# Program order on all four compute engines until the projections end, with three pieces of work one step later

## The chip, the cores and the metric

The kernel runs on one core of a Trainium2 chip. The metric is the device time of one launch in microseconds (us), as the median over several runs. The engines are TensorE (PE, matmuls; its weight loads are listed as PEld), VectorE (DVE), ScalarE (ACT), GpSimd (POOL) and SyncE (SP), whose queue issues nearly all transfers.

## The reference

One encoder layer over two sequences (256 and 2048 tokens, each with 16 learned meta tokens ahead). With z the input, in float32:

```python
h = rmsnorm(z, norm_w)
q, k, v, g_att, c_val, c_glu, g_conv = split(h @ w_in)      # 512,128,128,512,512,512,512
q, k = rmsnorm per head (64 wide)
att = windowed_gqa(q, k, v, sink) * silu(g_att)             # 8 heads, 2 KV heads, window 128, ALiBi, sink
cnv = conformer_conv(c_val, c_glu, ...) * silu(g_conv)      # GLU, depthwise conv of 31, layernorm, silu
y = z + concat(att, cnv) @ w_out
```

Each block of 128 queries sees its own block of keys, the block before and the one after, and the 16 meta keys. The meta tokens' own outputs are dropped.

## The kernel before

**Blocks and precision.** The 2304 tokens are 18 blocks of 128 (2 of the short sequence, 16 of the long one), in six groups of three. Float32 products are made of two parts: each operand is split into a high half (a cast on ACT) and a low half (a subtraction on DVE), and a product takes three matmuls (high x high, high x low, low x high).

**Stage 1, projections.** Two chunks of three groups. For each chunk the columns of `w_in` are taken unit by unit (256 columns): the convolution's units, its gate, the attention gate, keys and values, then two units of q. The last unit of the second chunk is q's second half for blocks 9 to 17: nine projections of 24 matmuls each (`proj_te`, L790 to L804; the matmul is L796). Each is followed by `head_norm` (L892: a squaring on ACT, L897; a sum on DVE, L898; two POOL instructions at L122 and L123 that make the reciprocal root `rqq`), and by `fin` in `q_group` (L914: DVE multiplies by `rqq`, L916, and a store to DRAM follows two ticks later). The convolution's taps on DVE and a layernorm for it are worked off beside the projections and are done before this last unit.

**Stage 2, attention and output.** Attention runs in steps `(s, slot)`, eight slots for each block (`slot_step`, L567). A slot issues: a bank of four transposes of finished probabilities (`bank`, L433, of the block before), two output products (`outproj`, from slot 14 on), and one pair of score matmuls S (`scores`, L354). Behind S come, one tick later, the bias and row minimum on DVE (`bias_max`, L382), two ticks later the exponential on ACT (`expo`, L394), and after the fourth S of a KV head, three ticks later, `norm` (DVE L406 and L407, POOL L408 and L417). A bank is split by ACT (L451, `ph`) and DVE (L452, `pl`) one tick later, and multiplied with V (`pv`, L475) two ticks later; `pvm` and `pd` in the text are the product with the meta values and POOL's operand for it (L462). `merge` puts the results together; it waits until `rest` exists, a tile that takes the place of the last projection weights.

**The clock of ticks.** `later(k, f)` appends f to a list that is run k ticks on; `tick()` ends a projection or a slot, and runs what is due, in the order in which it was appended. So the Python program fixes an emission order for every engine.

**The overlap, around the change.** `attention_open()` (L218) is called ahead of the last unit, when block 9's projection is next. It opens the pools of stage 2, loads q, k, bias, sink and the first `w_out` rows, clears three tiles on POOL, and computes `nsnk` from the sink on DVE (L250). Then `spread(b)` (L600) runs after each of the nine projections: after the second it issues `q_prep(0)` (transposes of q, tagged qT; the split by ACT L347, L348 and DVE L349, L350 a tick later); after each of the third to ninth it runs two slots, 14 in all: the eight of block 0, then the first six of block 1, with block 0's banks. After the third to the eighth it calls `split_wo`, which casts two halves of a row block of `w_out` on ACT (L301), subtracts on DVE (L302) and a tick later loads the row block two further on (L287).

**What sets the order.** The scheduler orders each engine's instructions at build time by its own estimate of when each is ready, unless told otherwise. `manual_schedule(engines)` makes the named engines issue what is emitted within it in emission order. From `attention_open()` on to the end of the projections this holds for `MAN1`, which is POOL alone; afterwards for `MAN2`, POOL and PE. `keep_in_program_order` pins a single instruction behind the one emitted before it on its engine. SP's queue is the scheduler's throughout.

**PSUM.** Four tags of two buffers each. The nine last projections take tags a, b, d, c, d, c, d, c, d; S takes a, transposes take b, attention's products c, output products d.

Of the kernel before, what the change touches and what calls it, by code (L numbers as in the profile page):

```python
# [14 lines left out]
ALU = mybir.AluOpType  # L15
# [31 lines left out]
W0 = 3  # L47
LN_WAIT = (9, 2)
LTAGS = "abdcdcdcd"
MAN1 = {mybir.EngineType.Pool}  # L50
MAN2 = {mybir.EngineType.Pool, mybir.EngineType.PE}
QSLOT = 6
MSLOT = 0
# [22 lines left out]
def hymba_kernel(  # L76
# [13 lines left out]
    nc = tc.nc  # L90
# [45 lines left out]
    def later(k, f):  # L136
        due.setdefault(clock[0] + k, []).append(f)
# [34 lines left out]
    phase = [1]  # L172
# [40 lines left out]
    pool, cst, kw, wo, wo_slot, sbs, wraws = {}, {}, [], {}, {}, [], {}  # L213
# [4 lines left out]
    def attention_open():  # L218
# [4 lines left out]
        cst['man'] = man  # L223
        man.enter_context(tc.manual_schedule(engines=MAN1))
        ap = att_pools.enter_context(tc.tile_pool(name="ap", bufs=2, side="right", reuse_waits="tile"))
# [57 lines left out]
    def load_raw(n):  # L283

        for nh in range(2):
            raw = wraws[n, nh] = pool["a"].tile([P, 512], F32, tag="woraw", name=f"woraw{n}_{nh}", bufs=4)
            tc.keep_in_program_order(nc.sync.dma_start(raw, w_out[OUT_ORDER[n]][:, 512 * nh : 512 * nh + 512]))  # L287

    def split_wo(n):

        e = OUT_ORDER[n]
        for hl in range(2):
            idx = 2 * n + hl
            if idx % 3 == 0:
                slot = idx // 3
                wo_slot[slot] = xp.tile([P, ND, 400], F32R, tag=("xh", "xl")[slot % 2], name=f"wo{slot}")
            flat = wo_slot[idx // 3].rearrange("p a n -> p (a n)")
            wo[e, hl] = flat[:, D * (idx % 3) : D * (idx % 3) + D]
        for nh in range(2):
            hi, lo = (wo[e, hl][:, 512 * nh : 512 * nh + 512] for hl in range(2))  # L300
            tc.keep_in_program_order(nc.scalar.copy(hi, wraws[n, nh]))  # L301
            tc.keep_in_program_order(nc.vector.tensor_tensor(lo, wraws[n, nh], hi, op=ALU.subtract))  # L302
        if n + 2 < 8:
            later(1, lambda: load_raw(n + 2))

    def load_ga(b):
        gat[b] = pool["b"].tile([P, 4, P], F32, tag="ga", name=f"ga{b}", bufs=1)
# [28 lines left out]
    def q_prep(b):  # L336
        pt = psum.tile([P, 4, P], F32, tag="b", name=f"qT{b}")
        for j in range(4):
            pin(b == 0 and j == 0)(nc.tensor.transpose)(pt[:, j, :], qt[b][:, j, :], ident)
        q2 = pool["a"].tile([P, 4, 4, 2, QB], F32R, tag="q2", name=f"q2_{b}")  # L340
        q2t[b] = q2
        later(1, lambda: q_split(pt, q2))
# [83 lines left out]
    def plan(b):  # L426
        ks = ([0] if has_left(b) else []) + [1] + ([2] if has_right(b) else [])
        return [(k, 0) for k in ks] + [("m", 0)] + [(k, 1) for k in ks]
# [4 lines left out]
    def bank(b, k, kv):  # L433
        pt = psum.tile([P, 4, P], F32, tag="b", name=f"pT{b}_{k}_{kv}")
        if k == "m":
            for i in range(KV):
                nc.tensor.transpose(pt[:, i, :], pmt[b][:, i].rearrange("p a h m -> p (a h m)"), ident)
        else:
            for hl in range(4):
                nc.tensor.transpose(pt[:, hl, :], sbt[b, kv][:, hl, KCOL[k] : KCOL[k] + P], ident)  # L440

        def split():
            if k == "m":
                ph = pool["a"].tile([P, KV, P], F32R, tag="phm", name=f"phm{b}", bufs=1)
                nc.scalar.copy(ph, pt[:, 0:KV, :])
                nc.vector.tensor_tensor(ph[64:128], pt[64:128, 0:KV, :], ph[64:128], op=ALU.subtract)  # L446
                later(1, lambda: spread_meta(b, ph))
                return
            ph = pool["a"].tile([P, 4, P], F32R, tag="ph", name=f"ph{b}_{k}_{kv}", bufs=3)
            pl = pool["a"].tile([P, 4, P], F32R, tag="pl", name=f"pl{b}_{k}_{kv}", bufs=3)  # L450
            nc.scalar.copy(ph, pt)  # L451
            nc.vector.tensor_tensor(pl, pt, ph, op=ALU.subtract)  # L452
            pv_st[b, k, kv] = (ph, pl)

        later(1, split)
        later(3 if k == "m" else 2, lambda: pv(b, k, kv))

    def spread_meta(b, ph):

        pd = pool["a"].tile([P, KV, 4, P], F32R, tag="pd", name=f"pd{b}", bufs=1)  # L460
        for kv in range(KV):
            nc.gpsimd.tensor_tensor(  # L462
                pd[:, kv],
                ph[:, kv : kv + 1, :].to_broadcast([P, 4, P]),
                cst["msk"].unsqueeze(2).to_broadcast([P, 4, P]),
                op=ALU.mult,
            )
        pv_st[b, "m"] = pd

    def pv_mm(b, kv, lhs, hs, start, stop):  # L470
        if start:
            opj[b, kv] = psum.tile([P, 4, P], F32, tag="c", name=f"O{b}_{kv}")
        o = opj[b, kv]
        for i, t in enumerate(hs):
            nc.tensor.matmul(o, lhs, t, start=(start and i == 0), stop=(stop and i == 1))  # L475

    def pv_meta(b, kv, stop):
        pin(stop)(nc.tensor.matmul)(
            opj[b, kv], cst["vm"][:, kv, :], pv_st[b, "m"][:, kv], start=False, stop=stop
        )  # L480

    def pv(b, k, kv):
        if k == "m":
            pv_meta(b, 0, True)
            later(1, lambda: merge(b, 0))
            return
        ks = [x for x, y in plan(b) if y == kv and x != "m"]
        first, last = k == ks[0], kv == 1 and k == ks[-1]
        pv_mm(b, kv, vt[b - 1 + k][:, kv, :], pv_st[b, k, kv], first, last)
        if kv == 1 and first:  # L490
            pv_meta(b, 1, False)
        if last:
            later(1, lambda: merge(b, 1))

    def merge(b, kv):
        if "rest" not in cst or (kv == 1 and b not in att):
            return later(1, lambda: merge(b, kv))
        o = opj[b, kv]
        if kv == 0:
            att[b] = pool["b"].tile([P, 4, P], F32, tag="at", name=f"at{b}")  # L500
            mix[b, 1] = (rest_part(2 * (b % 2)), rest_part(2 * (b % 2) + 1))
        at = att[b]
        pr = slice(2 * kv, 2 * kv + 2)
        tmp = pool["b"].tile([64, 4, P], F32, tag="tmp", name=f"tmp{b}_{kv}", bufs=1)
        nc.scalar.copy(tmp, o[64:128])
        for par in range(2):
            nc.vector.tensor_tensor(
                at[64 * par : 64 * par + 64, pr, :].rearrange("p a (i q) -> p a i q", q=QB),
                o[0:64].rearrange("p i (a c q) -> p c a i q", a=2, c=2)[:, par],
                tmp.rearrange("p i (a c q) -> p c a i q", a=2, c=2)[:, par],  # L510
                op=ALU.add,
            )
        nc.gpsimd.tensor_tensor(at[:, pr, :], at[:, pr, :], gat[b][:, pr, :], op=ALU.mult)

        def fin():
            mh, ml = mix[b, 1]
            nc.scalar.copy(mh[:, pr, :], at[:, pr, :])
            nc.vector.tensor_tensor(ml[:, pr, :], at[:, pr, :], mh[:, pr, :], op=ALU.subtract)

        later(2, fin)  # L520
# [77 lines left out]
    spread_n = [0]  # L598

    def spread(b):  # L600

        spread_n[0] += 1
        if spread_n[0] == QP:
            q_prep(0)
        upto = EARLY * max(0, spread_n[0] - QP) // (9 - QP)
        while len(slots) > len_all - upto:
            slot_step(*slots.pop(0))
        if 3 <= spread_n[0] <= 8:
            split_wo(spread_n[0] - 3)
        if spread_n[0] == 4:  # L610
            load_mix(0)
        if spread_n[0] == 5:
            load_ga(0)
# [21 lines left out]
    if True:  # L635
# [273 lines left out]
        def q_group(ws, qi, g, after):  # L909
            for b in range(3 * g, 3 * g + 3):  # L910
                ps = proj_te(ws, g, blk_local(b)[1], P)
                rq = head_norm(ps, P, 4, f"q{qi}_{b}")

                def fin(ps=ps, rq=rq, b=b):  # L914
                    qs = gp.tile([P, 4, HD], F32, tag="qs", name=f"qs{qi}_{b}")
                    nc.vector.tensor_tensor(  # L916
                        qs,
                        ps[:, :UW].rearrange("p (h e) -> p h e", e=HD),
                        rq.unsqueeze(2).to_broadcast([P, 4, HD]),
                        op=ALU.mult,  # L920
                    )
                    store(qd[b, :, UW * qi : UW * qi + UW], qs.rearrange("p h e -> p (h e)"))

                owe(340)
                later(1, fin)
                tick(24 * 110)
                after(b)

# [132 lines left out]
        for i, (c, u, g) in enumerate(items):  # L1061
# [36 lines left out]
            if c == 0 and u in U_GA:  # L1098
                for k3 in range(3):
                    k = 10 + 3 * (3 * (u - U_GA[0]) + g) + k3  # L1100
# [78 lines left out]
```

## Time and profile before

| | us |
|---|---|
| median of 3 runs | 977.79 (976.96 to 979.07) |
| profiled execution | 974.97 |
| its span | 972.8 |
| PE busy in the span | 947.0 (97%) |
| DVE busy | 754.1 (78%) |
| ACT busy | 422.5 (43%) |
| POOL busy | 340.6 (35%) |

The profile shows one execution. Its page lists busy time, a strip of 40 slices of 24.3 us with the busy share of each engine in tenths and the granted TensorE clock, the chain of work that ended last, and the costliest groups of instructions. By the chain of work PE holds 92% of the span; the chain is made of projections (L780, L796), output products (L551) and the attention's matmuls. A timeline row gives start, duration, engine, line and operation, and in brackets how long the engine stood idle before it and what released it. A row of waits gives total, count and longest.

The nine projections of the last unit begin at about 576 us and the last one ends at 616 us.

### The profile page before, as it was taken

The numbers are of one execution on the slowest core, as the hardware profiler recorded it, in microseconds if no ns is written. First come the engines' busy times: TensorE is split into PE (matmuls) and PEld (weight loads), VectorE is DVE, ScalarE is ACT, GpSimd is POOL, SyncE is SP. The second block draws the span as 40 slices with busy tenths as digits, with TensorE's granted clock in tenths as the row PEclk, the third lists the DMA queues.
The fourth block names the chain that finished last, engine by engine and source line by source line (L and its number), as shares of the span: only waits on it lengthen the run. The fifth ranks groups of instructions, "written<-read, shape, count | busy, mean of one in ns | idle before, by whom it ended". The sixth has DMA issues, their size and how long they took to land.

```text
span 972.8 us, 16221 instructions
## 1 busy us (share of the span) xinstructions
PE 947.0 (97%) x5721; PEld 886.3 (91%) x5721; DVE 754.1 (78%) x1261; ACT 422.5 (43%) x1156; POOL 340.6 (35%) x541
## 2 busy tenths in 40 slices
PE   5999999999999999999999998899999999999998
PEld 4999999999999999999999998678888888888886
DVE  4659999998977799999993555867777677767773
ACT  7521121343566710111113455656666666656661
POOL 5600000364467300000002443855445444445442
PEclk9999999999999999999999998999999999999999
DMA  9653354775635221233335639854555445544422
GB/s 332 229 188 117 117 178 172 265 287 189 225 123 174 76 91 74 86 128 136 127 135 179 207 111 258 257 156 126 166 163 164 125 148 170 171 135 127 138 78 76
DMA packets 113872, 155.75 MB, mean 160 GB/s; under 512 B 10592, under 2 KB 77296, under 8 KB 113792
## 3 DMA queue, kind: packets, MB, share of 16 engines
q1 hardware_dynamic: 113648, 154.11, 48.1%
q0 software_dynamic: 144, 0.62, 0.4%
q8 instruction: 45, 0.74, 0.3%
q14 instruction: 35, 0.29, 0.1%
HBM read 101.00 MB, written 54.31 MB: 160 GB/s over the span
## 4 chain that ended last, share of the span: by engine, by line
PE 92%; DMA 2%; DVE 2%; SPq 1%; POOL 1%; issue 1%; ACT 1%; DVEq 0%; POOLq 0%; ACTq 0%
PE pj L780 42%; PE y L551 20%; PE pj L796 14%; PE O L475 5%; PE pT L440 4%; PE S L327 3%; PE O L327 1%; PE lnt L184 1%; DMA wraw<-in_w_in 1%; PE lnu L203 1%; PE qT L327 1%; DMA v<-vd 1%; DMA qd<-qs 1%; DVE wo L302 0%; DVE sb L382 0%
## 5 line engine op out<-in xcount | busy, mean ns | idle before, releaser
L780 PE MATMUL pj<-xh,ws 128*128 128x384 f32 (+1 forms) x1536 | 396.9, 339 | 2.4 <-ACT xh L711 2.4
L863 DVE SCALAR_TENSOR_TENSOR y<-us,cw,y 128x1167 f32<-128x1167 f32 x240 | 328.9, 1425 | 0.6
L780 PEld LDWEIGHTS pj<-xh,ws 128*128 128x128 f32 x1536 | 282.4, 189 | 2.7 <-ACT xh L711 2.7
L780 PE MATMUL pj<-xl,ws 128*128 128x384 f32 (+1 forms) x768 | 262.0, 341 | 0.0
L551 PE MATMUL y<-wo,rest 128*128 128x512 f32 x648 | 173.6, 405 | 0.0
L796 PE MATMUL pj<-ws,xh 128*128 128x256 f32 (+1 forms) x880 | 165.6, 286 | 2.2 <-ACT es L403 1.4
L780 PEld LDWEIGHTS pj<-xl,ws 128*128 128x128 f32 x768 | 144.8, 189 | 0.6 <-DVE xl L720 0.5
L796 PEld LDWEIGHTS pj<-ws,xh 128*128 128x128 f32 (+1 forms) x880 | 137.5, 189 | 3.5 <-ACT sb L394 1.6
L551 PEld LDWEIGHTS y<-wo,rest 128*128 128x128 f32 x648 | 115.2, 189 | 20.4
L796 PE MATMUL pj<-ws,xl 128*128 128x256 f32 (+1 forms) x440 | 125.0, 284 | 0.0
L394 ACT ACTIVATE sb<-sb,nm 128x304 f32<-128x304 f32 (+4 forms) x144 | 77.1, 535 | 63.6 <-DVE nm L382 61.7
L452 DVE TENSOR_TENSOR pl<-pT,ph 128x512 fp32r<-128x512 f32 x100 | 68.5, 685 | 31.8 <-ACT ph L451 31.0
L888 ACT ACTIVATE go<-pj 128x384 f32<-128x384 f32 x48 | 23.6, 491 | 153.9 <-PE pj L780 143.9
L382 DVE CUSTOM_DVE_ANT_0 sb<-S,bias,small 128x304 f32<-128x304 f32 (+4 forms) x144 | 73.1, 511 | 16.0 <-PE S L327 14.9
L796 PEld LDWEIGHTS pj<-ws,xl 128*128 128x128 f32 (+1 forms) x440 | 83.2, 189 | 0.2
L122 POOL TENSOR_SCALAR ssk<-ssk 128x2 f32<-128x2 f32 x18 | 6.4, 354 | 210.9 <-ACT sqk L902 210.8
L417 POOL TENSOR_SCALAR sb<-sb,es 128x304 f32<-128x304 f32 (+4 forms) x144 | 72.1, 519 | 3.5
L451 ACT CAST ph<-pT 128x512 fp32r<-128x512 f32 x100 | 58.0, 581 | 32.8 <-PE pT L440 32.0
L327 PEld LDWEIGHTS S<-kw,q 128*128 128x128 f32 x288 | 53.0, 188 | 13.1 <-DVE nm L382 1.4
L327 PE MATMUL S<-kw,q 128*128 128x304 f32 (+4 forms) x288 | 61.9, 299 | 0.6 <-DVE nm L382 0.6
L440 PE MATMUL pT<-ident,sb 128*128 128x128 f32 x400 | 60.4, 272 | 1.2 <-DVE phm L446 1.1
L122 POOL TENSOR_SCALAR ssq<-ssq 128x4 f32<-128x4 f32 (+2 forms) x55 | 26.4, 480 | 98.1 <-ACT xn L649 76.7
(118 smaller groups left out, 1280.5 us busy)
## 6 DMA issues: line engine op xcount, KB each, us to landing
wd<-ws SPq DMA_DIRECT2D x36, 512.0 KB, 5.7
ws<-wd SPq DMA_DIRECT2D x36, 512.0 KB, 5.3
wraw<-in_w_in SPq DMA_DIRECT2D x52, 256.0 KB, 5.9
xn<-in_z SPq DMA_DIRECT2D x18, 512.0 KB, 5.4
gd<-go SPq DMA_DIRECT2D x48, 192.0 KB, 2.3
yo<-in_z SPq DMA_DIRECT2D x36, 256.0 KB, 4.5
out_y<-yo SPq DMA_DIRECT2D x36, 256.0 KB, 2.7
kw<-kd SPq DMA_DIRECT2D x16, 512.0 KB, 4.6
```

Source lines behind the costliest of these rows:

```text
L327: r = f(*a, **k)
L382: nc.vector.tensor_tensor_reduce(out=sb[:, n, c0:c1], in0=ps[:, 0:w], in1=cst["bias"][:, kv, n, c0 - QB * n : c1 - QB * n], scale=1.0, sca ...
L394: nc.scalar.activation(sb[:, n, c0:c1], sb[:, n, c0:c1], AF.Exp, bias=nm[:, n : n + 1], scale=-1.0, accum_out=rs[:, n : n + 1],)
L417: nc.gpsimd.tensor_scalar(sb[:, k, a0:a1], sb[:, k, a0:a1], es[:, k : k + 1], 1.0, op0=ALU.mult, op1=ALU.mult)
L440: nc.tensor.transpose(pt[:, hl, :], sbt[b, kv][:, hl, KCOL[k] : KCOL[k] + P], ident)
L451: nc.scalar.copy(ph, pt)
L452: nc.vector.tensor_tensor(pl, pt, ph, op=ALU.subtract)
L475: nc.tensor.matmul(o, lhs, t, start=(start and i == 0), stop=(stop and i == 1))
L551: nc.tensor.matmul(ps, mh[mi][:, e % 4, :], wo[e, wi][:, cols], start=(e == 4 and k == 0), stop=(e == 3 and k == 2),)
L780: nc.tensor.matmul(ps[:, :n], ws[:, d, wi, P * half_i : P * half_i + P], x[xi][:, d, o : o + n], start=(k == 0), stop=(k == 3 * ND - 1),)
L796: nc.tensor.matmul(ps[:rows, :UW], x[xi][:, d, o : o + rows], ws[:, d, wi, :], start=(k == 0), stop=(k == 3 * ND - 1),)
L863: nc.vector.scalar_tensor_tensor(y[:, yo + o0 : yo + o1], u[:, o0 + k : o1 + k], cw[:, j, k : k + 1], y[:, yo + o0 : yo + o1], op0=ALU.mul ...
```

## The change

`MAN1` becomes all four compute engines, so that from `attention_open()` until the projections end PE, ACT, DVE and POOL all issue in emission order. Four pieces of work are moved in that order:

- In `split_wo` the low half of the first 512 columns is emitted one tick after the cast and that of the second two ticks after; the next load of `w_out` rows is emitted with the second low half. In `spread`, `split_wo` is called ahead of the two slots instead of behind them.
- The products of block 0's probabilities with V (`pv`) come three ticks after the bank instead of two.
- In `q_group`, `fin` comes `phase[0]` ticks after the projection: one as before in the earlier units, two in the last unit, where `phase[0]` is 2.

```diff
-MAN1 = {mybir.EngineType.Pool}
+MAN1 = {getattr(mybir.EngineType, e) for e in ("Pool", "PE", "Activation", "DVE")}
...
             tc.keep_in_program_order(nc.scalar.copy(hi, wraws[n, nh]))
-            tc.keep_in_program_order(nc.vector.tensor_tensor(lo, wraws[n, nh], hi, op=ALU.subtract))
-        if n + 2 < 8:
-            later(1, lambda: load_raw(n + 2))
+
+            def low(nh=nh, hi=hi, lo=lo):
+                tc.keep_in_program_order(nc.vector.tensor_tensor(lo, wraws[n, nh], hi, op=ALU.subtract))
+                if nh == 1 and n + 2 < 8:
+                    load_raw(n + 2)
+
+            later(1 + nh, low)
...
-        later(3 if k == "m" else 2, lambda: pv(b, k, kv))
+        later(3 if k == "m" or b == 0 else 2, lambda: pv(b, k, kv))
...
         upto = EARLY * max(0, spread_n[0] - QP) // (9 - QP)
+        if 3 <= spread_n[0] <= 8:
+            split_wo(spread_n[0] - 3)
         while len(slots) > len_all - upto:
             slot_step(*slots.pop(0))
-        if 3 <= spread_n[0] <= 8:
-            split_wo(spread_n[0] - 3)
...
-                later(1, fin)
+                later(phase[0], fin)
```

## The prediction

> **What bounds the kernel now.** I read the strip of 40 slices first, then busy time by stretch, then waits by engine, then the timeline of the stretch that stood out.
>
> ```profile
> PE   5999999999999999999999998899999999999998
> DVE  4659999998977799999993555867777677767773
> PEclk9999999999999999999999998999999999999999
> ```
>
> ```profile
> 577.00:597.00 20.00, 20.00 (x173) 20.00 (x172) 6.44 (x18) 8.55 (x20) 9.35 (x30) 1.00 0.67 186
> 597.00:617.00 20.00, 15.49 (x91) 13.25 (x90) 15.09 (x48) 14.20 (x45) 7.16 (x14) 0.83 1.02 329
> 617.00:637.00 20.00, 15.01 (x72) 11.15 (x71) 17.84 (x37) 13.05 (x31) 14.84 (x19) 0.91 0.64 192
> 637.00:657.00 20.00, 19.91 (x109) 16.76 (x108) 13.28 (x38) 11.57 (x33) 11.04 (x19) 1.00 0.50 145
> ```
>
> The columns are stretch, length, then busy time of PE, weight loads, DVE, ACT and POOL, the granted clock, DMA share and GB/s. PE bounds the program. Its one weak place is 597 to 637: it is idle 4.51 + 4.99 = 9.5 us and the clock falls. That is exactly the stretch that the change reorders. Afterwards PE is full, so the end moves by what PE loses before 637, and by nothing else.
>
> ```profile
> PE pj L796 <- ACT es L403: 1.4, 1, 1.4
> PE pT_m L437 <- POOL pm L408: 2.1, 1, 2.1
> 597.00:599.00 2.00, 0.68 (x7) 0.48 (x5) 1.38 (x3) 1.36 (x5) 0.00 (x0) 1.00 0.85 223
> 599.00:601.00 2.00, 1.74 (x10) 1.20 (x10) 2.00 (x10) 1.33 (x4) 0.00 (x0) 1.00 0.98 259
> 601.00:603.00 2.00, 0.84 (x4) 0.46 (x3) 0.45 (x4) 1.96 (x6) 0.00 (x0) 0.57 1.02 277
> 603.00:605.00 2.00, 1.81 (x8) 1.84 (x9) 2.00 (x7) 2.00 (x10) 0.00 (x0) 0.50 1.01 341
> 633.00:635.00 2.00, 0.55 (x3) 0.15 (x2) 2.00 (x7) 0.55 (x3) 0.00 (x0) 1.00 0.74 206
> 635.00:637.00 2.00, 1.36 (x7) 1.15 (x8) 0.47 (x2) 0.92 (x3) 1.72 (x4) 1.00 0.36 130
> 603.19 0.55 PE L796 MATMUL pj<-ws,xh 128*128 128x256 f32 x1 [1.35 <-ACT es L403]
> 608.19 0.28 PE L796 MATMUL pj<-ws,xh 128*128 128x256 f32 x1
> 582.18 0.39 ACT L897 ACTIVATE sqq<-pj 128x256 f32<-128x256 f32 x1 [0.56 <-PE pj L796]
> 584.96 0.38 ACT L897 ACTIVATE sqq<-pj 128x256 f32<-128x256 f32 x1 [2.39 <-PE pj L796]
> 587.80 0.38 ACT L897 ACTIVATE sqq<-pj 128x256 f32<-128x256 f32 x1 [2.46 <-PE pj L796]
> ```
>
> Each squaring of q (L897) follows the end of one projection: at full clock one takes 587.80 - 584.96 = 2.84 us. Block 16's took 603.19 to 608.3, some 5.0 us, at a granted clock of 0.50: 2.2 us lost. The second dip (0.91 over 617 to 637 is 1.8 us of clock, a part of it while PE idled anyway) I put at 1.5. So PE loses **13.2 us** now: 9.5 idle, 3.7 clock. No edit to the order can gain more.
>
> **The change, part by part.** The program order of PE, read from the loops, is: projections 9, 10, qT of block 0, projection 11, two S, projection 12, two S, 13, two S, 14, S, qT of block 1, S, 15, then a bank of transposes before each S, with first products after projection 16 and 17. Now the scheduler ran ahead with projections: the first S is at 593.49, when 9 to 13 and most of 14 are done.
>
> *(a) Program order on PE and DVE, the beginning.*
>
> ```profile
> 582.02 0.42 SPq L281 DMA_DIRECT2D q<-qd  x1
> 583.13 0.62 SPq L237 DMA_DIRECT2D small<-in_sink  x1
> DMA to landing us min/median/max: 2.7/2.9/5.9
> small<-in_sink SPq DMA_DIRECT2D x1, 1.0 KB, 4.0
> 587.38 1.05 POOL L123 TENSOR_TENSOR rqq<-ssq,half 128x4 f32<-128x4 f32 x1
> 588.51 0.19 POOL L122 TENSOR_SCALAR ssq<-ssq 128x4 f32<-128x4 f32 x1
> 589.88 0.20 POOL L122 TENSOR_SCALAR ssq<-ssq 128x4 f32<-128x4 f32 x1
> 588.60 0.58 ACT L347 CAST q<-qT 64x512 fp32r<-64x512 f32 x1 [0.41 <-PE qT L327]
> 589.13 0.16 DVE L250 TENSOR_SCALAR small<-small 128x2 f32<-128x2 f32 x1
> 590.29 0.69 DVE L349 TENSOR_TENSOR q<-qT,q 64x512 fp32r<-64x512 f32 x1
> 593.49 0.59 PE L327 MATMUL S<-kw,q 128*128 128x176 f32 x4
> ```
>
> Projection 10 ends at 582.18. qT stands next on PE, and its q is only issued at 582.02; with 2.9 to land (the third row is q's) PE waits until about 585.0, **2.8 to 3.2 us** idle. Now qT runs at 588 behind ready projections and waits for nothing. Projection 11 then ends at 588.3, and S must wait for q's split. On DVE the first instruction of the ordered stretch is L250, which waits for the sink: 583.13 + 4.0 = 587.15. Behind it stand the sums of squares of 9 and 10 (0.36 us each from start to start), then the norm of 9, which needs POOL's two instructions. POOL, which is busy with its own opening until 587.1 today too, starts them at about 587.8 and takes 1.37 a block (588.51 and 589.88 are starts of successive ones), so block 10's is ready at 590.5. Then DVE does the norm of 10 and two subtractions for q (1.4): S at **592.4**. PE idles 592.4 - 588.3 = **4.1**. Sum of (a): **7.3 us** lost where PE loses nothing today. If q landed sooner the same wait would merely move behind projection 11: only projections 10 and 11 and qT (6.2 us) stand before an S that POOL and DVE can't release earlier than about 591.8. Bounds 6.5 and 8.3.
>
> *(b) The seven steps from S to S.*
>
> ```profile
> L302 DVE TENSOR_TENSOR wo<-woraw,wo 128x512 fp32r<-128x512 f32 x16 | 12.2, 776 | 0.1
> L382 DVE CUSTOM_DVE_ANT_0 sb<-S,bias,small 128x176 f32<-128x176 f32 (+3 forms) x18 | 7.5, 439 | 2.9 <-PE S L327 2.8
> L452 DVE TENSOR_TENSOR pl<-pT,ph 128x512 fp32r<-128x512 f32 x6 | 4.1, 679 | 0.0
> 612.42 0.68 DVE L302 TENSOR_TENSOR wo<-woraw,wo 128x512 fp32r<-128x512 f32 x1
> 613.02 0.41 DVE L916 TENSOR_TENSOR qs<-pj,rqq 128x256 f32<-128x256 f32 x1
> 613.36 0.15 DVE L406 TENSOR_TENSOR es<-es,rs 128x4 f32<-128x4 f32 x1
> ```
>
> Starts lie closer than durations: a 512-wide subtraction holds DVE 0.61, a norm 0.36, a bias with its read 0.40. In a plain step DVE does sum of squares, norm, low, bias, low, bias: 0.36 + 0.36 + 2 x 0.61 + 2 x 0.40 = 2.74. But between sum of squares and norm lies POOL: 1.37 and three hand-overs of some 0.07 (its row at 588.51 starts 0.08 after the one at 587.38 has ended), 1.56. "One step later" puts the norm into the tick of the first slot, and between the two places DVE has nothing but, every other block, the 0.24 of es. So DVE waits 1.56 (blocks 12, 14, 16) or 1.32 (13, 15, 17, in parts, for ACT's exponential too): 8.7 us. With 1.9 at the first step, where DVE has caught up and waits for projection 12, and 1.7 of small ones (ACT's casts of the banks) DVE waits 12.2 beside 23.0 of work (6 sums 2.2, 7 norms 2.5, 12 lows 7.3, 14 biases 5.6, q's split 1.3, es 0.7, 4 pl 2.4, phm 0.4, mcl 0.6): from 592.2 to 627.4. PE's own work from the first S to the fourteenth is 6 x 2.84 + 14 x 0.36 + qT and banks 2.8 + products 1.85 = 26.7; each S needs the bias two before it (tag a has two buffers) and each product its pl, so the fourteenth ends not at 619.1 but at 624.8: **5.7 us** idle, the largest 1.6 before the meta product (POOL's pd behind cn and the norm of 16) and 1.2 before a first product. Bounds 2 (DVE's waits half hidden) and 9.
>
> *(c) Lows later, loads of w_out with them.* ACT's casts move ahead of the two slots, each low one tick behind its cast, so DVE never waits for ACT there; the lows cost DVE the same 0.61. The load of raw n + 2 is issued with the second low: after the low at 594.2 it lands by 600.7 even at the slowest 5.9 above, its cast comes at 601.6. It hides by 0.9; if SP's queue holds it behind a store of qs, itself a step later now, that cover is gone and a step costs up to 1 us more. A gain is bounded by a bias that no longer stands behind its low, 0.6 once. I take 0, nearest to the landing rows; bounds -0.6 and 3.
>
> *(d) First products one step later.* They then stand behind projection 16 instead of a bank's split: included in (b). Merges wait for `rest` anyway, which needs projection 17 done. So 0; bounds -0.5 and 0.5, one product's time on PE.
>
> *(e) The tail.* At 624.8 PE still waits 2.0 for the last pl; 1.4 of products y fit in. DVE is 2.7 us of work behind today's (two lows and the merges, done by 627.4 now). Today PE waits 2.1 at 633 to 635.6; with the arrears I take the same kind of wait at 0.4. Sum **1.0**, bounds 0 and 3.
>
> ```profile
> 622.55 1.52 DVE L534 TENSOR_TENSOR mcl<-cn,mch 128x512 fp32r<-128x512 f32 x1
> 633.32 0.68 DVE L534 TENSOR_TENSOR rest<-cn,rest 128x512 fp32r<-128x512 f32 x1
> ```
>
> The same subtraction took 0.84 more while POOL was at pd; in the new order mcl and a low again stand beside pd. **1.0**, bounds 0 and 2.2 (the 16 lows' mean 776 against 690, and mcl).
>
> *(f) The clock.* Today it fell to half where PE had been busy 3.3 of 6 us (597 to 603), and did not at 633 to 637, busy 1.9 of 4. In (a) PE is busy 3.3 of the 10.2 us from 582.2 to 592.4, which is nearer to the first. I take one projection at half, as block 16's: **2.2**. Bounds 0 and 4.4 (two of them).
>
> [...]
>
> **Sum.** New losses 7.3 + 5.7 + 1.0 + 1.0 + 2.2 = 17.2, today's 13.2: **+4.0 us**. The profiled execution took 974.97, 2.8 below the median 977.79; applied to the median, **981.8 us**.
>
> **Rivals.**
> *Cover wins (faster).* Six projections, 17 us, now stand among the S instead of before them. If the steps run at PE's pace because DVE's wait for POOL is hidden, the fourteenth S ends at 619.1 and (b) is 0; without dip and tail the loss is 7.3 + 1.0: 8.3 - 13.2 = -4.9, **972.9 us**. It decides once a plain step takes under 3.56 us on DVE (2.74 of work leaves 0.8 for a wait that POOL's rows put at 1.56). For it: DVE is idle 13.6 of 20 us before 597. Against: POOL's 1.37 a block. Chance 0.24.
> *No dip, arrears absorbed.* (f) is 0 and (e) 0: 14.0 - 13.2 = +0.8, **978.6**. Chance 0.23.
> *Queues slip.* SP holds a load in three steps and the clock falls twice: 4.0 + 3 + 2.2, **987**. Chance 0.07.
> The forecast: 0.46. The scheduler keeping today's order is no rival: the order is forced.
>
> **Numbers.** A measurement tells about 0.2% from nothing, here 2.0 us: same is 975.8 to 979.7. Faster 0.24; same 0.23; slower 0.46 + 0.07 = 0.53. The range takes in half of the faster case and the bounds of (b) and (f), 974 to 986; the forecast's own range is 979.8 to 985.
>
> **What would show it.** (a): qT right behind projection 10 with a wait of about 3, first S near 592.4 behind projection 11, PE busy about 13 of 20 between 577 and 597. (b): DVE's norms waiting for POOL's rqq, in all 8 to 9 us; squaring of block 17 near 622.5. (f): a clock of 0.5 near 593. It is wrong if the norms don't wait, if the last squaring comes before 619, or if PE is full from 625 on with DVE's arrears gone.

## The result, and the profile after

| | before | after |
|---|---|---|
| median, same chip, 6 runs each (us) | 977.38 (975.25 to 979.1) | 982.05 (981.69 to 985.5) |
| profiled execution | 974.97 | 982.0 |
| its span | 972.8 | 980.2 |
| PE busy | 947.0 | 946.4 |

The ratio after to before is 1.0054, with a 95% interval of 1.0034 to 1.0074: slower by about half a per cent. The time predicted was 981.8. Line numbers are those of each run's own kernel (L916 before is L920 after). The profiled execution of before lies 2.4 below its median, that of after at its own, so the two traces lie 7.0 apart where the medians lie 4.7 apart; this matters below.

The strip of 40 slices, page of after, the rows of PE and DVE (the clock's row is the same as before):

```profile
PE   5999999999999999999999987799999999999998
DVE  4659999898978799999974544876777677767773
```

PE's weak place begins one slice earlier and is deeper (it was 8, 8 and is 8, 7, 7), and DVE, the engine that was meant to be fed in order, shows 5, 4, 4 where it had 5, 5, 5. Busy time by stretch, after, with the columns as before (PE, weight loads, DVE, ACT, POOL, clock, DMA share, GB/s):

```profile
577.00:597.00 20.00, 14.28 (x109) 13.89 (x108) 6.61 (x17) 8.77 (x21) 6.63 (x27) 0.91 0.72 199
597.00:617.00 20.00, 13.36 (x89) 12.47 (x88) 10.17 (x28) 8.26 (x23) 6.51 (x10) 0.83 0.92 304
617.00:637.00 20.00, 16.26 (x103) 13.44 (x103) 16.60 (x41) 13.47 (x36) 14.19 (x21) 1.00 0.41 126
637.00:657.00 20.00, 18.62 (x100) 15.33 (x99) 15.24 (x41) 12.86 (x36) 11.53 (x17) 1.00 0.54 159
```

PE now idles 5.7 + 6.6 + 3.7 + 1.4 = 17.5 us, against 9.6 before; the clock is 0.91 and 0.83 where it was 0.83 and 0.91. Multiply PE's busy time by the clock and add the four rows: 59.0 us of full-speed work after, 66.4 before (from the four rows quoted in the prediction). The difference, 7.5, is the difference of the spans, 7.4. So the whole loss is in these 80 us. The same sum for each kernel below tells its span to within 1.5 us.

Where PE waits, timeline of after, rows of PE with their waits (in brackets the idle time and what ended it):

```profile
584.31 1.11 PE L331 MATMUL qT<-ident,q 128*128 128x128 f32 x4 [2.72 <-DMA q<-qd]
592.21 0.67 PE L331 MATMUL S<-kw,q 128*128 128x176 f32 x4 [3.00 <-ACT wo L301]
602.52 0.73 PE L331 MATMUL S<-kw,q 128*128 128x176 f32 x2 [3.51 <-DVE nm L386]
615.57 0.49 PE L331 MATMUL S<-kw,q 128*128 128x272 f32 x2 [2.55 <-ACT sqq L901]
627.90 0.50 PE L331 MATMUL O<-pd,vm 128*128 128x512 f32 x1 [1.49 <-POOL pd L466]
```

The first, second and fifth were forecast, with their places. The third and fourth were not. Behind them stand two waits for transfers, on DVE and on ACT (after; SP's rows say when a transfer was issued):

```profile
601.06 0.42 DVE L920 TENSOR_TENSOR qs<-pj,rqq 128x256 f32<-128x256 f32 x1 [4.39 <-DMA qd<-qs]
590.23 4.10 SPq L257 DMA_DIRECT2D vm<-vmd  x8
596.80 0.85 SPq L159 DMA_DIRECT2D qd<-qs  x2
597.75 0.93 SPq L287 DMA_DIRECT2D woraw<-in_w_out  x2
605.86 0.99 SPq L287 DMA_DIRECT2D woraw<-in_w_out  x2
611.67 1.30 ACT L301 CAST wo<-woraw 128x512 fp32r<-128x512 f32 x2 [1.92 <-DMA woraw<-in_w_out]
612.88 0.57 ACT L351 CAST q<-qT 64x512 fp32r<-64x512 f32 x1
614.77 0.69 DVE L354 TENSOR_TENSOR q<-qT,q 64x512 fp32r<-64x512 f32 x1
```

The norm of block 12 writes its result `qs` into one of three buffers, the one that block 9's norm has filled. That norm ran at 588.75, but SP issued its store only at 596.80, behind the loads of attention's operands (`vm` from 590.23, then the next block's q, k and v); the store is done at 601.0. Until then DVE does nothing: behind the norm stand, in program order, the low halves and the two biases that the next S need, and PE runs out 599 to 602.5. Ten us on, ACT's cast waits for a row block of `w_out` whose load was issued at 605.86. Behind the cast stand, on ACT and then on DVE, the halves of block 1's q, which the ninth S needs: it starts at 615.57, 0.11 after the last of them ends. (The view names the squaring as what ended PE's wait, but that was done at 615.06. For the first S, too, it names a cast, one that ended at 592.10 together with the last half of block 0's q.)

A wait for the store alone isn't new. In the kernel before, DVE waited 2.42 for the same store, and later 1.55 for the next:

```profile
594.78 0.42 DVE L898 TENSOR_REDUCE ssq<-sqq 128x4 f32<-128x256 f32 x1
595.79 0.37 SPq L159 DMA_DIRECT2D qd<-qs  x1
597.62 0.42 DVE L916 TENSOR_TENSOR qs<-pj,rqq 128x256 f32<-128x256 f32 x1 [2.42 <-DMA qd<-qs]
```

What differs is where the norms stand. The first row is block 14's sum of squares; the scheduler put its norm at 613.02, behind twelve biases. After, that sum is at 609.34 and its norm at 611.17, with nothing between them.

Of DVE's waits, 585 to 640, after, those of the norms and of the low halves:

```profile
DVE qs L920 <- POOL rqq L123: 5.2, 6, 1.4
DVE qs L920 <- DMA qd<-qs: 4.4, 1, 4.4
DVE wo L304 <- ACT wo L301: 0.7, 1, 0.7
```

### The profile page after: what moved, and what is told of

It reads as the page before. It is cut to its first block, busy times and chain, and to the rows that moved or that the text cites. A ratio compares the mean times of both kernels' runs of the same rounds, so it can differ in the third digit from the quotient of the medians.

```text
span 980.2 us, 16215 instructions
## 1 busy us (share of the span) xinstructions
PE 946.4 (97%) x5721; PEld 886.5 (90%) x5721; DVE 755.5 (77%) x1261; ACT 422.4 (43%) x1156; POOL 340.6 (35%) x541
## 4 chain that ended last, share of the span: by engine, by line
PE 87%; DVE 4%; DMA 3%; ACT 2%; issue 1%; SPq 1%; POOL 1%; POOLq 0%; DVEq 0%; ACTq 0%
PE pj L784 39%; PE y L555 19%; PE pj L800 13%; PE O L479 4%; PE pT L444 4%; PE S L331 3%; PE O L331 1%; DVE wo L304 1%; DMA wraw<-in_w_in 1%; PE lnt L184 1%; PE lnu L203 1%; PE qT L331 1%; DVE xt L698 1%; DMA v<-vd 1%; DVE sb L386 1%
## 5 line engine op out<-in xcount | busy, mean ns | idle before, releaser
L386 DVE CUSTOM_DVE_ANT_0 sb<-S,bias,small 128x304 f32<-128x304 f32 (+4 forms) x144 | 73.5, 511 | 13.7 <-PE S L331 12.6
L421 POOL TENSOR_SCALAR sb<-sb,es 128x304 f32<-128x304 f32 (+4 forms) x144 | 74.4, 534 | 3.6
```

Of the source, the lines that this page charges most:

```text
L386: nc.vector.tensor_tensor_reduce(out=sb[:, n, c0:c1], in0=ps[:, 0:w], in1=cst["bias"][:, kv, n, c0 - QB * n : c1 - QB * n], scale=1.0, sca ...
L421: nc.gpsimd.tensor_scalar(sb[:, k, a0:a1], sb[:, k, a0:a1], es[:, k : k + 1], 1.0, op0=ALU.mult, op1=ALU.mult)
```

## The experiments

Each was timed in five rounds against the kernel before on the same chip. The theory at the start: what costs the time is waits on DVE and ACT that program order turns into waits of everything behind them; the rival: the early wait of PE, 7.3 us by the prediction's step (a), which is the largest term of the sum.

**Which engine's order, and are the moves a part of it?** Four kernels, each with one line changed:

```diff
-MAN1 = {getattr(mybir.EngineType, e) for e in ("Pool", "PE", "Activation", "DVE")}
+MAN1 = {getattr(mybir.EngineType, e) for e in ("Pool",)}                        # e1_moves_only
+MAN1 = {getattr(mybir.EngineType, e) for e in ("Pool", "PE")}                   # e3_pe_pool
+MAN1 = {getattr(mybir.EngineType, e) for e in ("Pool", "Activation", "DVE")}    # e4_pe_free
# e2_order_only: the kernel before with the four engines in MAN1, and no work moved
```

> The three moves (low halves, q's norms, first products one step later) with POOL alone in program order. Theory 1, the loss comes from holding PE and DVE to program order: PE again runs ahead with the projections while S waits for q, no wait of 2.7 and 3.0 us at 581 to 592, and the time is that of before, 977.4 within 2. Rival, the moves themselves cost because lows, norms and loads come later: about 982, as the changed kernel.

> All four engines in program order, none of the three moves. Theory 1: the waits at 581 to 592 stay, DVE's wait between sum of squares and norm stays (no DVE work stood between the two places anyway), and in addition each low stands on DVE right behind its cast on ACT: 983 to 987, slower than the changed kernel by 1 to 5. Rival, the moves cost: faster than the changed kernel, 977 to 980.

> The moves, with PE and POOL in program order and ACT and DVE left to the scheduler. If the loss is PE's early order (waits 2.7 + 3.0 and the slow clock behind the first of them, 7.0 in all): 981 to 984, as the changed kernel, with both waits in the trace. If it is DVE's order (waits for POOL and, once, 4.4 for the store of q): 976 to 979, and the early waits are made good later.

> The moves, with ACT, DVE and POOL in program order and PE left to the scheduler. If the loss is PE's early order: 976 to 979, projections 12 to 14 run ahead of the first S. If it is DVE's order: 981 to 984, with DVE waiting for POOL's root and for the store as in the changed kernel while PE runs dry after 600.

| | median (us) | to before |
|---|---|---|
| before | 976.68 | |
| moves only | 975.61 (971.84 to 978.72) | 0.9991 [0.9973, 1.0009] |
| order only | 986.45 (985.87 to 987.35) | 1.0097 [1.0076, 1.0117] |
| moves, PE and POOL in order | 976.22 (973.85 to 978.84) | 0.9994 [0.9979, 1.0008] |
| moves, all but PE in order | 981.84 (979.29 to 983.94) | 1.0049 [1.0034, 1.0065] |

The moved work alone changes nothing; order alone costs 1.0%, nearly twice the change as made, so under program order the moves win some 0.43% back, about 4 us. With order alone DVE does not wait for a store at all between 585 and 640, but longer for POOL:

```profile
DVE qs L916 <- POOL rqq L123: 9.9, 7, 1.5
```

So with the four engines in order the wait for the store comes with the moves: none without them, 4.39 with them. In the kernel before, block 9's store leaves SP ahead of the next block's q (595.79 against 596.20); after, behind its q, k and v (596.80). With the moves alone DVE waits 2.4 for the store, and the time is that of before.

PE's order is free: with it alone (beside POOL) the time is that of before, without it that of after. PE does wait early there; windows and timeline of the kernel with PE and POOL in order:

```profile
577.00:597.00 20.00, 15.96 (x123) 15.58 (x123) 6.52 (x17) 7.86 (x17) 7.14 (x27) 0.91 0.66 182
597.00:617.00 20.00, 13.77 (x103) 13.40 (x102) 13.73 (x40) 13.42 (x38) 8.26 (x15) 0.91 0.88 289
617.00:637.00 20.00, 16.82 (x105) 14.05 (x103) 18.86 (x46) 14.73 (x38) 14.12 (x19) 1.00 0.66 216
585.16 1.11 PE L331 MATMUL qT<-ident,q 128*128 128x128 f32 x4 [2.79 <-DMA q<-qd]
```

It loses 5.5 us of full-speed work before 597 (20 - 15.96 x 0.91), where before it lost none. From 597 to 637 it then does 29.4 us of full-speed work, where the kernel before did 15.49 x 0.83 + 15.01 x 0.91 = 26.5. About half of the early loss comes back within 40 us by these two executions, and by the medians all of it. In the kernel before PE ran ahead with projections and then starved; here it starves first and has projections left for later. DVE, whose order is still the scheduler's, works 13.7 and 18.9 us of these stretches, where after it works 10.2 and 16.6.

**DVE or ACT?**

```diff
+MAN1 = {getattr(mybir.EngineType, e) for e in ("Pool", "DVE")}           # e5_dve_pool
+MAN1 = {getattr(mybir.EngineType, e) for e in ("Pool", "Activation")}    # e6_act_pool
```

> The moves, with DVE and POOL alone in program order; PE and ACT left to the scheduler. If DVE's order is what costs: 980 to 983, as the changed kernel, with norms waiting for POOL's root and once for a store. If ACT's order is what costs: 975 to 978.

> The moves, with ACT and POOL alone in program order; PE and DVE left to the scheduler. If DVE's order is what costs: 975 to 978, as with POOL alone. If ACT's order costs (squarings stand behind exponentials, casts behind loads of w_out): 980 to 983.

DVE and POOL in order: 982.65 (981.18 to 985.72), ratio 1.0065 [1.005, 1.0081], all of the loss. ACT and POOL: 978.98 (976.42 to 983.9), 1.0017 [1.0003, 1.0032], a third of it, with an interval that nearly reaches nothing. In the first of them PE is full until 597, so the early wait is gone and the time is the same; the waits of DVE are those of after. Windows and DVE's waits, DVE and POOL in order:

```profile
577.00:597.00 20.00, 20.00 (x172) 20.00 (x171) 7.06 (x18) 10.07 (x24) 7.87 (x29) 1.00 0.68 188
597.00:617.00 20.00, 13.00 (x82) 11.80 (x80) 11.40 (x32) 10.86 (x29) 7.96 (x14) 0.82 1.01 330
DVE qs L920 <- DMA qd<-qs: 5.5, 1, 5.5
DVE qs L920 <- POOL rqq L123: 5.1, 5, 1.5
```

By these two the rival falls: the early wait of PE is neither needed for the loss (DVE and POOL in order) nor enough for it (PE and POOL in order).

**Which of the waits?** Three kernels take one wait away each, with all four engines in order. The first gives the odd blocks' `qs` of the last unit another buffer (one of a tag that is idle then), so that six stores may be under way instead of three. The second runs q's norm three ticks after its projection, not two, so that POOL's root is there. The third loads row blocks 2 and 3 of `w_out` at the opening, into idle buffers, and each later one a step earlier.

```diff
-                    qs = gp.tile([P, 4, HD], F32, tag="qs", name=f"qs{qi}_{b}")
+                    if phase[0] == 2 and b % 2:                                                   # e7_qs_bufs
+                        qs = gp.tile([P, 384], F32, tag="go", name=f"qs{qi}_{b}")[:, : 4 * HD]...
+                    else:
+                        qs = gp.tile([P, 4, HD], F32, tag="qs", name=f"qs{qi}_{b}")
...
-                later(phase[0], fin)
+                later(2 * phase[0] - 1, fin)                                                      # e8_fin3
...
+        load_raw(2)                                                                               # e9_raw_ahead
+        load_raw(3)
...
+            p, tag = (pool["b"], "yo") if n in (2, 3) else (pool["a"], "woraw")
...
-                if nh == 1 and n + 2 < 8:
-                    load_raw(n + 2)
+                if nh == 1 and n in (0, 1, 4, 5):
+                    load_raw(n + 4 if n < 2 else n + 2)
```

> The changed kernel with six buffers for the normalised q instead of three (every other block takes a buffer of the gates, which lie idle then). DVE's one wait of 4.4 us at 596.7 for the store of block 9's q goes. If each of DVE's waits counts in full: 977 to 979. If the next wait (raw rows of w_out, POOL) takes its place: 980.5 to 982.5.

> The changed kernel with q's norms yet one step later, in the tick of the second slot, where a low half and a bias stand between the sum of squares and the norm. DVE's waits for POOL's root, 5.9 us in seven, fall below 2. If they set the end: 977 to 979.5. Rival: the stores move back as well, the wait of 4.4 us for the buffer grows, and the time stays at 981 to 984.

> The changed kernel with row blocks 2 and 3 of w_out loaded when attention opens, into the four buffers of the residual input, which lie idle then, so that blocks 4 and 5 are loaded two steps earlier too. ACT's waits for raw rows (1.9 us at 609 in the changed kernel) go. If this wait counts by itself: 979.5 to 980.5. If one of the waits in line merely takes over (store of q, POOL's root): 981 to 983.

| | median (us) | to before (976.33 to 976.36) |
|---|---|---|
| other buffers for `qs` | 982.7 (981.62 to 986.17) | 1.0068 [1.0053, 1.0083] |
| norm one tick later | 981.22 (980.98 to 984.98) | 1.0055 [1.0041, 1.007] |
| rows of `w_out` ahead | 985.23 (983.25 to 986.04) | 1.0091 [1.0071, 1.0112] |

Against the 1.0054 of after, none of the three gains anything, and the third is slower, though the two intervals just touch. Each took its own wait away, and another grew in its place. The waits of 585 to 640, first of the kernel with other buffers, then with the norm one tick later, then with the rows ahead:

```profile
DVE qs L925 <- POOL rqq L123: 7.1, 7, 1.9
DVE wo L304 <- ACT wo L301: 5.9, 2, 4.6
ACT wo L301 <- DMA woraw<-in_w_out: 8.5, 2, 6.1
```

```profile
DVE wo L304 <- ACT wo L301: 5.3, 4, 3.7
DVE qs L920 <- DMA qd<-qs: 3.6, 1, 3.6
ACT wo L301 <- DMA woraw<-in_w_out: 4.8, 3, 3.1
```

```profile
DVE qs L923 <- POOL rqq L123: 5.3, 6, 1.4
DVE qs L923 <- DMA qd<-qs: 5.3, 1, 5.3
ACT wo L304 <- DMA woraw<-in_w_out: 1.4, 1, 1.4
```

With the store's wait gone, the load of `w_out` becomes the long one (1.9 to 8.5), and DVE's low halves wait for ACT. With POOL's wait gone, both transfers stay. With the loads ahead, four more of them stand in front of the store in SP's queue, which issues it at 598.39 instead of 596.80, and its wait grows from 4.4 to 5.3; the 1.4 in its third row is the first row block's, at 590.67, while the wait at 611.67 is gone.

**All of them, and the two transfers without POOL.** The three edits together, in order on all four engines; the two edits on transfers without the norm's; and the two with POOL alone in order, to see what they are worth where the scheduler may go around a wait.

```diff
# e10_all_waits: the edits of e7_qs_bufs, e8_fin3 and e9_raw_ahead
# e14_two_waits: those of e7_qs_bufs and e9_raw_ahead
# e13_pool_raw:  those of e7_qs_bufs and e9_raw_ahead, and
+MAN1 = {getattr(mybir.EngineType, e) for e in ("Pool",)}
```

> Three removals at once in the changed kernel: raw rows ahead, six buffers for q's norms, norms yet one step later. All four engines stay in program order. If the loss is the sum of these waits of DVE and ACT, which stand in for one another when taken away singly: 975 to 978, as before. If it is program order as such (PE's 2.7 and 3.0 us at the beginning included): 980 to 983.

> The moves with POOL alone in program order, raw rows ahead and six buffers for q's norms. With ACT's waits for raw rows (4.9 us) and DVE's for the store (2.4) gone there: 972 to 975 if they were on the path, 975 to 978 if the scheduler's order already worked round them.

> The changed kernel, all four engines in program order, with the other buffers for the odd blocks' qs and the rows of w_out loaded ahead, but with q's norm two ticks after its projection again: the two DMA waits are taken away and DVE's wait for POOL's root (5.9 us in all in the changed kernel) stays. If the two DMA waits alone make the 0.5% (the theory): 975 to 977, as with all three edits. If the wait for POOL has a share of its own on DVE, which bounds the first steps: 979 to 981. If taking two waits only moves the time into the third, as each of the three edits did alone: 982.

| | median (us) | to before (976.36; the last 976.09) |
|---|---|---|
| all three, four engines in order | 974.74 (971.57 to 978.19) | 0.9985 [0.9969, 1.0001] |
| the two on transfers, POOL in order | 975.94 (971.99 to 978.35) | 0.9992 [0.9977, 1.0006] |
| the two on transfers, four engines in order | 978.39 (976.23 to 981.49) | 1.0024 [1.0013, 1.0035] |

Together the three edits take away the whole loss: 0.69% by the ratios, some 7 us. It may be faster than before as well, by 0.15%, but the interval takes in 1. The windows, with all three:

```profile
577.00:597.00 20.00, 14.28 (x120) 13.89 (x120) 7.78 (x21) 9.60 (x23) 7.62 (x28) 1.00 0.74 207
597.00:617.00 20.00, 17.86 (x139) 16.35 (x137) 16.03 (x43) 13.60 (x38) 12.51 (x20) 1.00 0.97 320
617.00:637.00 20.00, 16.89 (x89) 13.04 (x89) 16.89 (x44) 13.77 (x37) 13.27 (x19) 1.00 0.57 180
637.00:657.00 20.00, 19.91 (x108) 16.75 (x106) 14.02 (x40) 12.31 (x34) 9.17 (x15) 1.00 0.48 145
584.27 0.66 PE L334 MATMUL qT<-ident,q 128*128 128x128 f32 x4 [2.72 <-DMA q<-qd]
590.76 0.67 PE L334 MATMUL S<-kw,q 128*128 128x176 f32 x4 [3.00 <-issue]
```

The early waits, 2.72 and 3.00 us, are those of after to the hundredth, and 577 to 597 has the same 14.28 of PE. What differs most is 597 to 617: DVE does 16.0 us of work instead of 10.2 and PE 17.9 instead of 13.4. The clock stays at 1.00 throughout, which is in part luck: this execution took 971.58, the second fastest of 12 and 3.2 below the median. By the medians too, program order as such isn't the loss.

The pair on transfers fell between two of its expectations: it wins 0.30% (1.0054 to 1.0024), and the norm's tick on top of it another 0.39%. DVE's wait for POOL is still there in the pair, 6.0 us from 590 to 635:

```profile
DVE qs L928 <- POOL rqq L123: 6.0, 6, 1.9
```

The norm's tick is worth nothing while the transfers are late, and some 3.7 us once they aren't. So the three waits do not add up; I read it as the latest one counting, step by step, though the norm's tick was not paired with either transfer alone. And where DVE, ACT and PE are the scheduler's, taking the two transfer waits away is worth nothing (0.9992 against 0.9991 with the moves alone): its order, it seems, has other work to put there.

## Why the prediction was right, point by point

- **The time.** 981.8 against 982.05. The sum itself was +4.0 against the profiled execution, and against that after is 7.0 longer: the sum was some 3 us short, and was put on a median that lies 2.4 to 2.8 above the execution it was made from. The two errors cancelled; the sign and the rough size were right, the close hit was in part luck. Term by term the trace of after gives 21.0 us lost from 577 to 657 where the sum had 17.2: idle for (a) 5.7 (7.3 forecast), idle from the first S on 11.8 ((b) and (e): 7.7), clock 3.6 (2.2).
- **What PE loses before 657 is what the end moves by:** right, 7.5 by the windows against 7.4 of span.
- **(a)** Seen almost as forecast: qT behind projection 10 with a wait of 2.72 (2.8 to 3.2), L250 on DVE ending at 587.0 (587.15), the first S at 592.21 (592.4), PE busy 14.28 of 20 (about 13). The two waits make 5.7, below the bounds of 6.5 to 8.3, as projection 11 ran at a clock of 0.50 from 585 to 587 and ended at 589.2 instead of 588.3. As a piece of PE's idle time the mechanism was right. As a cause it was wrong: 7.3 us was booked as if it could not come back, and the kernel with PE and POOL in order has the wait and not the loss. What the step lacked, as I read the windows, is that DVE bounds the steps until about 635: a PE that starts S late still has projections to run when it would otherwise starve.
- **(b)** In the seven steps DVE's norms wait 4.1 us for POOL, not 8.7 (the 5.2 above hold block 9's 1.1 as well): blocks 14 and 16 wait 1.41 and 1.42 (1.56 forecast), 13, 15 and 17 0.49, 0.49 and 0.24 (1.32), as in two of them ACT's exponential, 0.54 each, and es stand before them; block 12's is hidden in its wait for the store. How 624.8 follows from DVE's 627.4 the prediction does not work out. The fourteenth S came at 631.4 and the squaring of block 17 at 628.69, not at 624.8 and 622.5, for a reason that (b) had not.
- **(c)** This is the term that was mis-sized. It was put at 0 with a bound of 3, and the clause on it was right: "if SP's queue holds it behind a store of qs, itself a step later now, that cover is gone". The queue did slip. The load that the prediction had going out behind the low at 594.2 was issued at 597.75, behind the loads and the store. And the store came first: the fourth norm of the unit needs the first one's buffer. That first norm ran at 588.75, as early as before (588.46), but in after its store stands behind the next block's loads in SP's queue (issued at 596.80; before, at 595.79). DVE's wait for it was 4.39 (2.42 before) and ACT's for the load 1.92, and PE's waits of 3.51 and 2.55 follow. The prediction counted the load in that queue but not the store's buffer. "Queues slip", the rival at 0.07, came in part: with the sum's 3 us, not with its 987.
- **(d)** nothing seen of it: 0 as forecast, though no run takes it by itself. The moves together cost nothing without the order (0.9991).
- **(e)** The tail is there: PE waits 0.40 and 0.90 for the last split at 632 and 633.6, and idles 1.4 in 637 to 657, where before it idled 0.1. The longer subtractions came as forecast, and ahead of pd beside POOL's cn too: the lows at 624.82 and 627.12 took 1.45 and 1.27 and mcl 1.50, where the nine lows from 592 to 619 took 0.68 or 0.69. Timeline of after:

```profile
624.42 1.30 POOL L530 TENSOR_TENSOR cn<-cn,gc 128x512 f32<-128x512 f32 x1
624.82 1.45 DVE L304 TENSOR_TENSOR wo<-woraw,wo 128x512 fp32r<-128x512 f32 x1
626.80 2.48 POOL L466 TENSOR_TENSOR pd<-phm,small 128x512 fp32r<-128x512 f32 x2 [1.09 <-DVE phm L450]
627.12 1.27 DVE L304 TENSOR_TENSOR wo<-woraw,wo 128x512 fp32r<-128x512 f32 x1
628.34 1.50 DVE L538 TENSOR_TENSOR mcl<-cn,mch 128x512 fp32r<-128x512 f32 x1
```

The low at 624.82 ends at 626.27, 0.55 after POOL's cn (625.72), which is nearly one low's own time of 0.68.

- **(f)** Two dips instead of one (2.2 forecast): clock 0.91 and 0.83, one behind the wait for qT (0.50 from 585 to 587) and one behind the 3.51 (0.50 from 603 to 607). Before had two as well (0.50 from 603 to 607 and from 623 to 625).
- **Cover wins** (the faster rival, 972.9) is what the kernel with all three edits does in part: its sums of squares on DVE follow each other by 3.3 to 5.7 us (594.77, 598.08, 602.04, 607.42, 613.14), only the first below the 3.56 from which that rival was to decide, and its median is 974.74.

What stays open: how much of after's loss is each wait's own, since they stand in for one another; what the norm's tick does with one transfer wait alone taken away; and whether the kernel with all three edits is faster than before.

## What to carry to other kernels

Before an engine is made to issue in program order, list for each instruction in that order every result it waits for, the store that must empty its buffer included, and when the queue that issues this store comes to it; an instruction that the scheduler used to put behind other work now holds all that stands behind it (here one norm held DVE for 4.39 us). When several such waits lie in one step, taking away one can show nothing (1.0068, 1.0055 and 1.0091 here, where all three gave 0.9985): try them together, then one at a time out of the full set. And a wait of the bounding engine that is seen in the profile is not yet the loss (PE waited 2.79 ahead of qT in the kernel with PE and POOL in order, at a ratio of 0.9994): ask whether the work it puts off fills a later gap.

## What the runs showed of the hardware

The same pattern of waits gave two clocks. After and the kernel with all three edits both idle on PE for 2.72 us ahead of qT and for 3.00 ahead of the first S. Windows of 2 us around qT, with the granted clock as the third number from the end, first after, then all three edits:

```profile
583.00:585.00 2.00, 0.69 (x3) 0.69 (x4) 0.00 (x0) 0.00 (x0) 0.95 (x3) 0.75 0.86 264
585.00:587.00 2.00, 2.00 (x11) 2.00 (x11) 0.19 (x2) 0.00 (x0) 1.51 (x18) 0.50 1.26 229
```

```profile
583.00:585.00 2.00, 0.73 (x6) 0.73 (x7) 0.00 (x0) 0.00 (x0) 0.99 (x4) 1.00 0.99 316
585.00:587.00 2.00, 2.00 (x19) 2.00 (x18) 0.47 (x3) 0.00 (x0) 1.47 (x17) 1.00 1.27 200
```

After fell to half speed on projection 11, the other did not, and neither fell behind the 3.00 us wait, though it is longer (1.00 from 591 to 595 in both). By these two executions a single gap of 2.72 or 3.00 us, then, doesn't tell whether the clock falls; a term for it belongs in the range more than in the sum. Over the 12 runs of the kernel with all three edits, the three with a mean granted clock of 0.999 took 971.57 to 972.19, the four with 0.995 took 975.8 to 978.19.

I had not expected a load that is made earlier to cost time: with the rows of `w_out` ahead, the kernel took 985.23, and its four loads were issued ahead of the one store that DVE stood waiting for. That wait grew by 0.9; the rest of what this kernel lost against after was not traced to a cause.
